# S5 mixer on one NeuronCore: tile 0's outputs with channels on the partitions, other gelu groups, earlier copies of u

## The chip, the cores and the metric

The kernel runs on one core of a Trainium2 chip. The metric is the device time of one execution in microseconds (us). All times below are us unless ns is written.

## What is computed

A trunk of two layers over x of [1, 256, 2048] in float32: differential attention and a squared-relu MLP, then the S5 mixer and a second MLP, each behind an RMS norm and added to the residual, and a final norm. The change touches the S5 mixer alone. Per group of 16 channels it is a diagonal complex state space of 64 states, read out and fed to a gated linear unit (GLU):

```
u = h.reshape(B, S, S5_GROUPS, S5_GROUP)
x_re, x_im = associative_scan(a, u @ b)        # over the 256 tokens
y = einsum(x_re, c_re) - einsum(x_im, c_im) + d_skip * h
g = gelu(y)
val, gate = split(g @ w_glu, 2)
out = val * sigmoid(gate)
```

## The kernel before

The 2048 channels are 16 tiles of 128 channels, and the 256 tokens are cut into 64 chunks of 4 tokens. Every tile is computed in a chunked form: matmuls give the end states of the chunks (`s5_e`, L1049, TensorE's line L1056), VectorE scans over the chunks (L1066) and makes the states that enter each chunk, and matmuls give the outputs (`s5_y`, L1078, TensorE's line L1089) from three terms: the tokens inside the chunk (`tt` with `u`) and the two parts of the entering state (`to` with `xp`). The tokens of a tile, `u`, are needed with token-in-chunk and channel on the partitions. `s5_u` (L1022) makes them for two tiles at a time: 8 matmuls onto one PSUM bank (TensorE, L1031) and 16 copies by ScalarE, each of 32 partitions and 128 elements (L1036).

`s5_y` puts the outputs into PSUM with 4 tokens x 32 channels on the partitions. So the gelu has to sort them: 16 instructions on ScalarE for a group of one or two tiles (L1096), each from one 32-partition strip to another and with a stride of 4 in what it writes. ScalarE then rounds the result (L1100), and VectorE makes the rounding's rest (`s5_rest`, L1107).

`glu_tile` (L1116, TensorE's line L1122) multiplies a tile's gelu, in full float32, with the first 512 columns of value and gate. It lags behind: tile 0 in step 2, tile 1 in step 3, none in step 4, and from step 5 on the tile three steps back.

The order of the work is written out by hand in `s5_phase` (L1129), and every engine keeps it. Step j issues: `s5_e` of tile j+1; `s5_rest` of tile j-3; in steps 0 and 1 eight warming matmuls (`keep_warm`, L320); `glu_tile`; the outputs of tile j; the copy of a decay table for tile j+4 (`s5_dk`, ScalarE, L1020); at the end of a group its gelus; in some steps `s5_u` of a later pair of tiles; and the fetch of tile j+4's tables on SP's queue (`s5_fetch`, L994). Before the steps, `s5_u` runs for tiles 4 to 7.

PSUM has 8 banks, given out in turn by `ring` (L88). In this phase the GLU sums hold four of them, `s5_y` takes banks 6 and 7 in turn, and `s5_e` and `s5_u` share banks 4 and 5, also in turn; a bank's new user waits until the old one has been read out:

```
rings["sd"], rings["y"] = [4, 5], [6, 7]
groups = [(0,), (1,), (2, 3), (4, 5), (6, 7), (8, 9), (10, 11), (12, 13), (14,), (15,)]
...
            if j in (2, 4, 6, 8):
                for _ in s5_u(j + 6, diag):
                    pass
```

The functions that the change touches, and what calls them:

Of the kernel before, what the change touches and what calls it, by code (L numbers as in the profile page):

```python
# [12 lines left out]
AF = mybir.ActivationFunctionType  # L13
# [3 lines left out]
P = 128  # L17
S = 256
# [4 lines left out]
KB = 4  # L23
# [12 lines left out]
L = 4  # L36
NCH = S // L
NJ = 16
Q = 4
# [18 lines left out]
def tile_trunk(  # L58
# [8 lines left out]
    act = nc.scalar  # L67
    pe = nc.tensor
# [11 lines left out]
    def nm(s):  # L80
        uid[0] += 1
        return f"{s}_{uid[0]}"
# [5 lines left out]
    def ring(kind):  # L88
        r = rings[kind]
        turn[kind] = (turn[kind] + 1) % len(r)  # L90
        return psum.tile([P, 512], F32, tag=f"bank{r[turn[kind]]}", name=nm(kind), bufs=1)
# [6 lines left out]
    def bank():  # L98
        return ring("sd")

    def tmp(shape, tag, bufs=None, dt=F32):
        if bufs is None:
            return sb.tile(shape, dt, tag=tag, name=nm(tag))
        return sb.tile(shape, dt, tag=tag, name=nm(tag), bufs=bufs)
# [10 lines left out]
    def tsc(o, a, s1, op0, s2=None, op1=None):  # L115
        if op1 is None:
            v.tensor_scalar(out=o, in0=a, scalar1=s1, scalar2=None, op0=op0)
        else:
            v.tensor_scalar(out=o, in0=a, scalar1=s1, scalar2=s2, op0=op0, op1=op1)
# [21 lines left out]
    def until(cond):  # L141
        while not cond():
            assert side
            pump()
# [79 lines left out]
    def new_accs():  # L224
        return [ring("acc") for _ in range(NT)]
# [94 lines left out]
    def keep_warm(n):  # L320

        if n == 0:
            return
        a = ring("acc")
        for _ in range(n):
            pe.matmul(a, x1[3].h[:, 0, 0:P], x1[3].h[:, 0:2], start=True, stop=True)

    def new_lhs(blk, tag):
        blk.hl = lp.tile([P, KB, 2, S], F32R, tag=tag, name=nm(tag))
        blk.h, blk.l = blk.hl[:, :, 0], blk.hl[:, :, 1]  # L330
# [659 lines left out]
    glu_lhs = [Lhs() for _ in range(NB)]  # L990
    tab, U, X, G = {}, {}, {}, {}
# [30 lines left out]
    def s5_u(j, diag=None, kind="sd"):  # L1022

        ps = ring(kind).rearrange("p (i s) -> p i s", s=S)
        for i in range(2):
            for t in range(NT):
                o, xs = ps[:, i, t * P:(t + 1) * P], xres[t][:, (j + i) * P:(j + i + 1) * P]
                if diag is None:
                    pe.transpose(o, xs, ident)
                else:  # L1030
                    pe.matmul(o, xs, diag[:, t], start=True, stop=True)  # L1031
        u = tmp([P, 2, Q, NCH], "vsb", bufs=4)
        pv = ps.rearrange("p i (k s) -> p i s k", s=L)
        for s in range(L):
            for q in range(Q):
                act.copy(u[32 * s:32 * s + 32, :, q], pv[32 * q:32 * q + 32, :, L - 1 - s])  # L1036
            yield s
        if diag is None:
            U[j] = u
        else:  # L1040
            U[j], U[j + 1] = u[:, 0], u[:, 1]

    def s5_scale(j, factor):
        u = U[j]
        uv = u.rearrange("p i q k -> p (i q) k")
        mult(uv, uv, factor[:, None, :].broadcast_to([P, 2 * Q, NCH]))
        U[j], U[j + 1] = u[:, 0], u[:, 1]

    def s5_e(j):  # L1049
        te, to, tt, ct = tab[j]  # L1050
        u, dk, xp = U[j], dks[j % 4], xps[j % 4]
        pe_ = bank().rearrange("p (i q k) -> p i q k", i=2, q=Q)
        for i in range(2):
            for q in range(Q):
                for h in (slice(0, GP), slice(GP, P)):
                    pe.matmul(pe_[h, i, q], te[:, i, q, h], u[:, q], start=True, stop=True)  # L1056
        sh = [P, 2, Q, NCH]
        tw = tmp([P, 2] + sh[1:], "c5")
        t1, t2 = tw[:, 0], tw[:, 1]
        mult(t1, pe_, ct[:, 0:1].broadcast_to(sh))  # L1060
        mult(t2, pe_, ct[:, 1:2].broadcast_to(sh))
        add(t1[:, 0], t1[:, 0], t2[:, 1])
        sub(t1[:, 1], t1[:, 1], t2[:, 0])
        zz = tmp(sh, "s2k", bufs=7)
        for i in range(2):
            v.tensor_tensor_scan(out=zz[:, i].rearrange("p q k -> p (q k)"), data0=dk.rearrange("p q k -> p (q k)"),  # L1066
                                 data1=t1[:, i].rearrange("p q k -> p (q k)"), initial=0.0,
                                 op0=ALU.mult, op1=ALU.add)
        n = NCH - 1
        shn = [P, 2, Q, n]  # L1070
        w1, w2 = tmp(sh, "s2k", bufs=7), tmp(sh, "s2k", bufs=7)
        mult(w1[:, :, :, 0:n], zz[:, :, :, 0:n], ct[:, 0:1, :, 0:n].broadcast_to(shn))
        mult(w2[:, :, :, 0:n], zz[:, :, :, 0:n], ct[:, 1:2, :, 0:n].broadcast_to(shn))
        sub(xp[:, 0, :, 1:], w1[:, 0, :, 0:n], w2[:, 1, :, 0:n])
        add(xp[:, 1, :, 1:], w1[:, 1, :, 0:n], w2[:, 0, :, 0:n])
        X[j] = xp

    def s5_y(grp):  # L1078

        n = len(grp)  # L1080
        py = ring("y").rearrange("p (j q k) -> p j q k", j=2, q=Q)
        for jj, j in enumerate(grp):
            te, to, tt, ct = tab[j]
            u, xp = U[j], X[j]
            for q in range(Q):
                terms = ((tt[:, q], u[:, q]), (to[:, 0, q], xp[:, 0, q]), (to[:, 1, q], xp[:, 1, q]))
                for m, (w_, d) in enumerate(terms):
                    for h in (slice(0, GP), slice(GP, P)):
                        pe.matmul(py[h, jj, q], w_[:, h], d, start=m == 0, stop=m == 2)  # L1089
            yield j  # L1090
            del U[j], X[j], tab[j]
        g = tmp([P, 2, S], "s2k", bufs=7)
        gv = g.rearrange("p j (k s) -> p j s k", s=L)
        for s in range(L):
            for q in range(Q):
                act.activation(gv[32 * q:32 * q + 32, 0:n, s], py[32 * s:32 * s + 32, 0:n, q], AF.Gelu_apprx_tanh)  # L1096
        blk, kk = glu_lhs[grp[0] // KB], grp[0] % KB
        if blk.h is None:
            new_lhs(blk, "x")
        act.copy(blk.h[:, kk:kk + n], g[:, 0:n])  # L1100
        for jj, j in enumerate(grp):
            G[j] = g[:, jj]
        rest.append((grp[-1], blk, kk, n, g))

    rest = []

    def s5_rest(j):  # L1107
# [21 lines left out]
    def s5_phase(norm):  # L1129
        until(lambda: norm.done)  # L1130
        act.activation(warm_act, warm_act, AF.Gelu_apprx_tanh)
        keep_warm(WARM[0])
        sel = wp.tile([P, 2, NT, P], F32, tag="wl", name="sel", bufs=LIVE)
        ar, diag = sel[:, 0], sel[:, 1]
        for t in reversed(range(NT)):
            tsc(ar[:, t], sela.rearrange("p s r -> p (s r)"), norm.rstd[:, t:t + 1], ALU.mult)
        for t in range(NT):
            act.activation(diag[:, t], ident, AF.Copy, scale=norm.rstd[:, t:t + 1])
        prs = bank()[:, 0:NCH]
        for t in range(NT):  # L1140
            pe.matmul(prs, ar[:, t], selb[:, t], start=(t == 0), stop=(t == NT - 1))
        keep_warm(WARM[1])
        s5_scale(0, prs)
        s5_scale(2, prs)
        s5_e(0)
        for j in (4, 6):
            for _ in s5_u(j, diag, "acc"):
                pass
        groups = [(0,), (1,), (2, 3), (4, 5), (6, 7), (8, 9), (10, 11), (12, 13), (14,), (15,)]
        ys = {}  # L1150
        for grp in groups:
            gen = s5_y(grp)
            for j in grp:
                ys[j] = (gen, j == grp[-1])
        glu = 0
        for j in range(NJ):
            if j + 1 < NJ:
                s5_e(j + 1)
            s5_rest(j - 3)
            if j < 2:  # L1160
                keep_warm(WARM[2])
            if j in (2, 3) or j >= 2 + LAG:
                if glu == 0:
                    A["v"], A["g"] = new_accs(), new_accs()
                glu_tile(glu)
                glu += 1
            gen, end = ys[j]
            next(gen)
            s5_dk(j + 4)
            if end:  # L1170
                for _ in gen:
                    pass
            if j in (2, 4, 6, 8):
                for _ in s5_u(j + 6, diag):
                    pass
            s5_fetch(j + 4)
            pump()
        while glu < NJ:
            prep(GLU0 + 16 + glu - NJ + LAG)
            glu_tile(glu)  # L1180
            glu += 1
        s5_rest(NJ)
# [212 lines left out]
```

## Time and profile before

| | |
|---|---|
| median of three runs | 2104.44 (2101.5 to 2106.57) |
| profiled execution, its time | 2101.04 |
| profiled execution, its span | 2099.3 |
| TensorE busy in the span | 2076.1 (99%) |
| VectorE, ScalarE, GpSimd busy | 1369.1, 1061.4, 122.9 |
| mean granted TensorE clock | 0.999 of full speed |

The profile's engines are PE (TensorE's matmuls), PEld (its weight loads), DVE (VectorE), ACT (ScalarE), POOL (GpSimd) and SP (the queue of most DMAs). A float32 matmul shows as two passes, so 24 matmuls are x48. `out<-in` names the tiles that an instruction writes and reads. A matmul's recorded duration contains its latency; what counts for the pace is the distance between starts, or the length of a whole row of passes.

### The profile page before, as it was taken

Reading aid. Unit: us, or ns where it says so; the run is one execution under the profiler, and the core shown is the slowest. Engines: PE = TensorE matmul, PEld = TensorE weight load, DVE = VectorE, ACT = ScalarE, POOL = GpSimd, SP = SyncE. Lnnn points to the kernel's source line nnn. Section 1 sums busy time; section 2 is a strip of 40 time slices with the busy share of each in tenths; the row PEclk is TensorE's granted clock in tenths of the full one; section 3 lists DMA queues with packets and bytes.
Section 4 is the critical chain, followed back from the end, with each engine's and each line's share of the span. In section 5 each row is a group of like instructions: output and inputs, shape, how many; then the busy total and the mean of one; then the engine's idle time right before and its main releaser. Section 6 shows DMA issues by size and latency. Waiting matters only on the chain.

```text
span 2099.3 us, 31788 instructions
## 1 busy us (share of the span) xinstructions
PE 2076.1 (99%) x12126; PEld 1763.8 (84%) x12126; DVE 1369.1 (65%) x2292; ACT 1061.4 (51%) x1640; POOL 122.9 (6%) x210
## 2 busy tenths in 40 slices
PE   8999999999999999999999999999999999999998
PEld 8899998888888888888887668888888888888886
DVE  5785656688678767767866865565556645645655
ACT  5545545555445444454566875444434434434443
POOL 2000200021021002100110000000000000000000
PEclk9999999999999999999999999999999999999999
DMA  7457765677776777687678765665565556555653
GB/s 244 157 193 241 248 178 184 214 229 267 237 240 233 273 238 222 225 276 235 208 266 310 274 215 187 200 201 199 189 195 189 189 193 191 178 204 181 200 192 131
DMA packets 230813, 452.57 MB, mean 216 GB/s; under 512 B 20818, under 2 KB 29348, under 8 KB 230660
## 3 DMA queue, kind: packets, MB, share of 16 engines
q1 hardware_dynamic: 217824, 415.29, 59.8%
q0 software_dynamic: 11440, 32.86, 4.9%
q10 hardware_dynamic: 1396, 2.39, 0.3%
q8 instruction: 95, 1.56, 0.3%
q14 instruction: 58, 0.48, 0.1%
HBM read 420.85 MB, written 41.68 MB: 220 GB/s over the span
## 4 chain that ended last, share of the span: by engine, by line
PE 91%; ACT 3%; DVE 3%; DMA 1%; issue 1%; SPq 0%; DVEq 0%; ACTq 0%
PE acc L265 21%; PE acc L201 15%; PE acc L202 15%; PE acc L203 15%; PE acc L269 11%; PE acc L1122 3%; PE acc L248 2%; PE acc L250 2%; PE acc L249 2%; DVE wl L113 1%; ACT wh L191 1%; PE y L1089 1%; ACT s2k L1096 1%; DMA raw<-in_a_w_in_dram 1%; ACT vsb L1036 1%
## 5 line engine op out<-in xcount | busy, mean ns | idle before, releaser
L113 DVE TENSOR_TENSOR wl<-raw,wh 128x1024 fp32r<-128x1024 f32 (+1 forms) x690 | 833.2, 1217 | 574.4 <-ACT wh L191 570.0
L191 ACT CAST wh<-raw 128x1024 fp32r<-128x1024 f32 (+1 forms) x690 | 712.9, 1047 | 631.0 <-PE acc L203 341.4
L201 PE MATMUL acc<-wh,x 128*128 128x512 f32 x832 | 326.8, 393 | 0.0
L203 PE MATMUL acc<-wh,x 128*128 128x512 f32 x832 | 324.0, 389 | 0.0
L202 PE MATMUL acc<-wl,x 128*128 128x512 f32 x832 | 324.0, 389 | 0.0
L265 PE MATMUL acc<-x,wh 128*128 128x512 f32 x1024 | 273.9, 394 | 2.8 <-DVE s2k L110 2.8
L265 PE MATMUL acc<-a,wh 128*128 128x512 f32 x1024 | 272.8, 393 | 0.0
L201 PE MATMUL acc<-wh,a 128*128 128x512 f32 x640 | 251.5, 393 | 0.0
L202 PE MATMUL acc<-wl,a 128*128 128x512 f32 x640 | 249.4, 390 | 0.1
L203 PE MATMUL acc<-wh,a 128*128 128x512 f32 x640 | 249.3, 390 | 0.0
L265 PEld LDWEIGHTS acc<-x,wh 128*128 128x128 f32 x1024 | 177.3, 189 | 28.9 <-DVE s2k L110 3.2
L265 PEld LDWEIGHTS acc<-a,wh 128*128 128x128 f32 x1024 | 177.3, 189 | 25.3 <-ACT s2k L1324 0.4
L203 PEld LDWEIGHTS acc<-wh,x 128*128 128x128 f32 x832 | 156.2, 188 | 32.9
L201 PEld LDWEIGHTS acc<-wh,x 128*128 128x128 f32 x832 | 156.3, 188 | 32.0 <-ACT vsb L1317 0.3
L202 PEld LDWEIGHTS acc<-wl,x 128*128 128x128 f32 x832 | 156.3, 188 | 31.8 <-issue 0.2
L269 PEld LDWEIGHTS acc<-a,wl 128*128 128x128 f32 x1024 | 152.8, 190 | 18.7
L269 PEld LDWEIGHTS acc<-x,wl 128*128 128x128 f32 x1024 | 152.4, 190 | 18.8
L269 PE MATMUL acc<-x,wl 128*128 128x256 f32 x1024 | 158.0, 282 | 0.0
L269 PE MATMUL acc<-a,wl 128*128 128x256 f32 x1024 | 157.5, 281 | 0.0
L248 PE MATMUL acc<-x,wh 128*128 128x256 f32 x512 | 148.4, 290 | 1.2 <-ACT wh L191 1.2
L249 PE MATMUL acc<-x,wh 128*128 128x256 f32 x512 | 145.4, 284 | 0.1
L250 PE MATMUL acc<-x,wl 128*128 128x256 f32 x512 | 145.5, 284 | 0.0
(246 smaller groups left out, 2105.8 us busy)
## 6 DMA issues: line engine op xcount, KB each, us to landing
raw<-in_mlp_w_dram SPq DMA_DIRECT2D x512, 512.0 KB
raw<-in_a_w_in_dram SPq DMA_DIRECT2D x94, 512.0 KB
raw<-in_b_w_glu_dram SPq DMA_DIRECT2D x64, 512.0 KB
raw<-in_a_w_out_dram SPq DMA_DIRECT2D x32, 512.0 KB
scr<-t POOLq DMA_DIRECT2D x32, 512.0 KB, 5.6
teo<-scr SPq DMA_DIRECT2D x32, 512.0 KB
t<-scr SPq DMA_DIRECT2D x16, 512.0 KB
pwr<-pwn SPq DMA_DIRECT2D x16, 256.0 KB
```

Of the source, the lines that this page charges most:

```text
L113: v.tensor_tensor(out=o, in0=a, in1=b, op=ALU.subtract)
L191: act.copy(h[:, sl], r[:, sl])
L201: pe.matmul(accs[t], lhs.h[:, k, ts], wh, start=first, stop=False)
L202: pe.matmul(accs[t], lhs.h[:, k, ts], wl, start=False, stop=False)
L203: pe.matmul(accs[t], lhs.l[:, k, ts], wh, start=False, stop=last)
L248: pe.matmul(o, wh[:, kk, cs], lhs.h[:, k], start=f and c % 2 == 0, stop=False)
L249: pe.matmul(o, wh[:, kk, cs], lhs.l[:, k], start=False, stop=False)
L250: pe.matmul(o, wl[:, kk, cs], lhs.h[:, k], start=False, stop=e and c % 2 == 1)
L265: pe.matmul(a[c], wh, lhs.hl[:, k].rearrange("p i s -> p (i s)"), start=first, stop=False)
L269: pe.matmul(a[c][:, S:], wl, lhs.h[:, k], start=False, stop=last)
L1036: act.copy(u[32 * s:32 * s + 32, :, q], pv[32 * q:32 * q + 32, :, L - 1 - s])
L1122: pe.matmul(accs[t], g[:, t * P:(t + 1) * P], raws[i][:, kk], start=j == 0, stop=j == NJ - 1)
```

## The change

Tile 0's outputs get a function of their own, `s5_y_direct`. Its matmuls have 32 columns of the stationary operand and write 32 channels x 64 chunks, for each of 4 tokens and 4 strips of channels; so channels lie on the partitions, and a single gelu over 128 partitions and 256 elements puts the tokens in order. Tiles 2 and 3 become groups of their own. `s5_u` for tiles 8 to 15 moves from steps 2, 4, 6, 8 to steps 1, 3, 5, 7, behind the outputs and gelus of that step.

```diff
+    def s5_y_direct(j):
+        te, to, tt, ct = tab[j]
+        u, xp = U[j], X[j]
+        py = ring("y")[:, 0:S].rearrange("p (s k) -> p s k", s=L)
+        for s in range(L):
+            cs = slice(32 * s, 32 * s + 32)
+            for q in range(Q):
+                terms = ((tt[:, q], u[:, q]), (to[:, 0, q], xp[:, 0, q]), (to[:, 1, q], xp[:, 1, q]))
+                for m, (w_, d) in enumerate(terms):
+                    pe.matmul(py[32 * q:32 * q + 32, s], w_[:, cs], d, start=m == 0, stop=m == 2,
+                              tile_position=(0, 32 * q))
+        yield j
+        del U[j], X[j], tab[j]
+        g = tmp([P, 2, S], "s2k", bufs=7)
+        act.activation(g[:, 0].rearrange("p (k s) -> p s k", s=L), py, AF.Gelu_apprx_tanh)
...
+        act.copy(blk.h[:, kk:kk + 1], g[:, 0:1])
+        G[j] = g[:, 0]
+        rest.append((j, blk, kk, 1, g))
...
-        groups = [(0,), (1,), (2, 3), (4, 5), (6, 7), (8, 9), (10, 11), (12, 13), (14,), (15,)]
+        groups = [(0,), (1,), (2,), (3,), (4, 5), (6, 7), (8, 9), (10, 11), (12, 13), (14,), (15,)]
...
-            gen = s5_y(grp)
+            gen = s5_y(grp) if grp[0] else s5_y_direct(0)
...
-            if j in (2, 4, 6, 8):
-                for _ in s5_u(j + 6, diag):
+            if j in (1, 3, 5, 7):
+                for _ in s5_u(j + 7, diag):
```

## Rows read from the trace of the kernel before

**Rows 1.** Windows view, S5 phase: stretch, length, busy time per engine, granted clock.

```profile
1129.70:1249.80 120.10, 115.27 (x1500) 75.93 (x1499) 94.44 (x182) 97.27 (x291) 0.00 (x0) 1.00 0.68 238
```

**Rows 2.** Chain of waits, S5 phase: start, length, engine, tile, line, instructions merged.

```profile
1175.77 1.15 PE sd L1056 x32
1176.92 3.63 PE acc L1122 x8
1180.55 1.55 PE y L1089 x48
1182.10 1.09 PE sd L1031 x8
1183.19 1.08 PE sd L1056 x32
```

**Rows 3.** Timeline of TensorE: start, length, line, tiles, shapes, [idle before <-releaser].

```profile
1146.89 0.62 PE L1089 MATMUL y<-bc,teo 128*64 128x64 f32 x8 [0.36 <-issue]
...
1151.27 3.70 PE L1122 MATMUL acc<-raw,s2k 128*128 128x512 f32 x8 [1.78 <-ACT s2k L1096]
...
1170.52 3.70 PE L1122 MATMUL acc<-raw,s2k 128*128 128x512 f32 x8 [2.15 <-ACT s2k L1096]
```

**Rows 4.** The same timeline: passes of the outputs now.

```profile
1142.07 0.29 PE L1089 MATMUL y<-vsb,t 128*64 128x64 f32 x4
1142.18 0.40 PE L1089 MATMUL y<-bc,teo 128*64 128x64 f32 x8
```

**Rows 5.** The same timeline: passes on 32-column strips, in the set-up of the tables.

```profile
1043.50 0.43 PE L927 MATMUL sd<-c,t 128*32 128x64 f32 x16
```

**Rows 6.** Timeline of ScalarE, steps 0, 1 and 3 to 5.

```profile
1146.57 4.64 ACT L1096 ACTIVATE s2k<-y 32x64 f32<-32x64 f32 x16
1151.25 0.40 ACT L1100 CAST x<-s2k 128x256 fp32r<-128x256 f32 x1
1151.56 0.39 ACT L1020 COPY s1k<-rr 128x252 f32<-128x252 f32 x1
...
1163.91 6.55 ACT L1096 ACTIVATE s2k<-y 32x128 f32<-32x128 f32 x16 [1.57 <-PE y L1089]
1170.50 0.62 ACT L1100 CAST x<-s2k 128x512 fp32r<-128x512 f32 x1
1171.02 0.40 ACT L1020 COPY s1k<-rr 128x252 f32<-128x252 f32 x1
1171.44 4.28 ACT L1036 COPY vsb<-sd 32x128 f32<-32x128 f32 x16
1175.74 0.40 ACT L1020 COPY s1k<-rr 128x252 f32<-128x252 f32 x1
```

**Rows 7.** One line's instructions (L466, 1257 to 1264): count, duration in ns min/median/max, shapes.

```profile
L466 ACT ACTIVATE a<-sd,gT x4: 474/475/476, 1258.5 to 1262.6; 128x256 fp32r<-128x256 f32 x4
```

**Rows 8.** Waits, 1120 to 1275: who waited for whom, us in total, times, longest.

```profile
PEld acc L201 <- ACT vsb L1317: 0.3, 1, 0.3
```

**Rows 9.** End of the program: TensorE's last matmul, then windows (granted clock third from last).

```profile
2089.48 0.39 PE L203 MATMUL acc<-wh,x 128*128 128x512 f32 x1
...
2092.00:2094.00 2.00, 0.00 (x0) 0.00 (x0) 1.71 (x6) 0.93 (x2) 0.75 (x1) 1.00 0.00 0
2094.00:2096.00 2.00, 0.00 (x0) 0.00 (x0) 0.28 (x1) 0.00 (x0) 0.00 (x0) 0.51 0.85 313
```

**Rows 10.** Timeline of TensorE at the program's start.

```profile
7.85 0.58 PE L248 MATMUL acc<-x,wh 128*128 128x256 f32 x1 [1.24 <-ACT wh L191]
...
9.60 0.41 PE L248 MATMUL acc<-x,wh 128*128 128x256 f32 x1
9.81 0.41 PE L249 MATMUL acc<-x,wh 128*128 128x256 f32 x1
...
12.17 0.28 PE L248 MATMUL acc<-x,wh 128*128 128x256 f32 x1
12.29 0.28 PE L249 MATMUL acc<-x,wh 128*128 128x256 f32 x1
```

More of the change, by code (lines that the diff above doesn't have):

```diff
@@ L1103, in s5_y @@
         rest.append((grp[-1], blk, kk, n, g))
+    def s5_y_direct(j):
[13 more added lines that the diff above has]
+        act.activation(g[:, 0].rearrange("p (k s) -> p s k", s=L), py, AF.Gelu_apprx_tanh)
+        blk, kk = glu_lhs[j // KB], j % KB
+        if blk.h is None:
+            new_lhs(blk, "x")
+        act.copy(blk.h[:, kk:kk + 1], g[:, 0:1])
+        G[j] = g[:, 0]
+        rest.append((j, blk, kk, 1, g))
     rest = []
```

## The prediction

> **What bounds the kernel now.** I first read the windows view over the S5 phase, from its first warming matmul to the first matmul of the next product: 120.1 us, of which TensorE is busy 115.3, ScalarE 97.3 and VectorE 94.4 [rows 1]. TensorE sets the pace, but with under 5 us to spare: whatever delays it comes out at the end of the phase, and what follows is a chain of matmuls, so a shift here moves the end of the program by as much.
>
> Next the chain of waits in this stretch, to see what a step is made of. A plain step on TensorE is the state matmuls of the next tile ("e", L1056, 1.08), the GLU product of an older tile (L1122, 3.63), the outputs ("y", L1089, 1.55) and, in four steps, the transposes of a pair of tiles ("u", L1031, 1.09) [rows 2]. Then TensorE's timeline, for where it stands still: 0.36 before y of tile 1, 1.78 before the first GLU product, 2.15 before the third [rows 3]. Both long waits end with a gelu. Removing everything that these rows show is worth 4.3 us, 0.2% of the time, which is also about what a measurement of this kernel can tell from no change.
>
> **The change, part by part.**
>
> *Outputs of tile 0.* Removed are 48 passes (24 matmuls, two passes each) in 1.55; added are 96 passes (48 matmuls) onto strips of 32 columns of the array. In the outputs of now, 4 passes take 0.29 and 8 take 0.40 [rows 4]: passes alternate between the two halves, so 4 more passes are 2 more rounds, 55 ns a round. The kernel has passes on 32-column strips in one place, L927: 16 passes in 0.43 [rows 5], but there neighbours go to different strips. In the new loop the six passes of one sum follow one another on the same strip, then come six on the next. If passes start in program order, as they do in all these rows, only the last of six overlaps with the first of the next: 5 rounds of 55 ns and some 10 ns to move on, 0.29 for each of 16 sums, 4.6 in all. The bounds are four strips fully in parallel (24 rounds, 1.3) and no overlap (96 rounds, 5.3). I take 4.6, since program order is what the rows show: 3.05 more than now. Nothing covers it: TensorE works in order, and e of tile 2, the warming matmuls and y of tile 1 stand behind it.
>
> By the Trainium skill ("TensorEngine Tiling", Theoretical Speedup) a stationary operand of 32 columns or fewer allows up to a fourfold gain, as tiles run independently. By that rule the new outputs take the lower bound and the sum falls by 3.3.
>
> *One gelu for tile 0.* Removed are 16 gelus of 32x64, 4.68 from the first to the cast behind them [rows 6]; added is one of 128x256. The nearest row is a scaled copy of the same shape out of PSUM, 0.475 [rows 7]; the gelus, which write with a stride as the new one does, go from 4.64/16 for 64 elements to 6.55/16 for 128 [rows 6], 1.9 ns an element, which gives 0.65 for 256. Either way ScalarE gains about 4.0. The gelu of tile 1 doesn't start 4 us earlier for it, as it waits for y of tile 1, which the longer y of tile 0 pushes back. The first GLU product loses its wait of 1.78, since its gelu is done long before.
>
> *Single gelus for tiles 2 and 3.* Two times 16 gelus of 32x64 in place of 16 of 32x128: 2 x 4.68 + 2 x 0.31 against 6.59 + 0.52 [rows 6], 2.9 more on ScalarE, but tile 2's are done a step earlier, so the third GLU product loses its 2.15. The outputs of tiles 0 to 3 now take a bank each; every y finds its bank's gelu finished.
>
> *The copies of u one step earlier.* This is the part that decides. The transposes of a pair of tiles go into one of two PSUM banks that they share, in turn, with e of every tile. After u of step j comes e of tile j+2 in the other bank and e of tile j+3 in u's own: it has to wait until ScalarE has copied all of u out. Before, u stands in steps 2, 4, 6, 8, behind the step's y, and in steps 4, 6 and 8 no gelu of that step is ahead of its copies. Even so there is little room: the copies of step 4 run from 1171.44 to 1175.72 [rows 6], and e of tile 7, the next in that bank, starts at 1175.77 [rows 2]. That a matmul waits for ScalarE to read out its bank is also seen where the next product waits for the eviction of the values [rows 8].
>
> After, u stands in steps 1, 3, 5 and 7, which all end a group: the gelus of that step come first on ScalarE's queue, they wait for the y just issued, and the copies wait behind them. From the end of y ScalarE needs gelu + cast + copies: 6.59 + 0.52 + 4.28 = 11.4 for a pair, 4.68 + 0.31 + 4.28 = 9.3 for a single tile [rows 6]. TensorE meanwhile has only u, one e, one GLU product and one y: 1.09 + 1.08 + 3.63 + 1.55 = 7.35; behind step 3 there is no GLU product (step 4 has none), so 3.7 [rows 2]. New waits of TensorE: step 1, 9.3 - 7.35 = 1.95 (before e of tile 4); step 3, 5.6 (tile 6); steps 5 and 7, 4.05 each (tiles 8 and 10); 15.7 in all. Everything on TensorE is queued behind these e, y included, so ScalarE can't work ahead either. VectorE's share is hidden: it waits for the same e. Moved with u are only its 8 passes and 16 copies; SP's and POOL's queues pass unchanged, and the fetches issued per step have a step or more in hand.
>
> *The sum without the clock:* 15.7 + 3.05 - 4.3 = +14.5 (between +11.1 and +15.2 by the bounds of the outputs).
>
> *The clock.* TensorE has not stood still for 5.6 us in this phase. At the end of the program the granted clock is still 1.00 in the stretch up to 2094 and 0.51 in the next, with the last matmul at 2089.48 [rows 9]: it falls to the lower of its levels (1.2 of 2.4 GHz) some 4 us behind the last work. After the 2.15 of now it doesn't fall: the phase reads 1.00 throughout [rows 1]. So the wait of 5.6 is likely to bring a fall, those of 4.05 stand on the edge. What one costs is bounded below by nothing and priced by the program's start: identical matmuls follow each other at 0.21 until about 11.6 and at 0.12 behind [rows 10], from 7.85 on 3.7 us of work, half of it lost: 1.9. I count one fall: +16.3 or so.
>
> By the Trainium skill ("TensorE: Matmul & The Clock Gate", HAM oscillation) a loop with idle gaps between its bursts of matmuls can run each burst at half rate. By that rule the three long gaps each cost a fall, and the sum is 3.8 higher; the trace bears out the fall at its end, and no gap in its middle is long enough to test it.
>
> The profiled execution took 2101.04, the median of three runs is 2104.44. The sum gives 2117.3 against the first and 2120.7 against the second; I predict a median, so 2120.7.
>
> **Rivals.**
> - *The waits come, the clock holds:* +14.5, 2118.9. For it: single waits under some length are harmless now. Against it: 5.6 is longer than the lag seen at the end of the program. Chance 0.22.
> - *The clock falls in each of the three long waits:* 14.5 + 3 x 1.9 = +20.2, 2124.6. For it: 4.05 is close to the lag at the end. Chance 0.15.
> - *Not slower: u is copied out in time.* The place is e of tiles 4, 6, 8 and 10. If the bank is free when TensorE comes by, only the outputs (+3.05) and the lost waits (-4.3) remain: -1.2, 2103.2; with the outputs at their lower bound -4.5, 2099.9. It decides from the point where gelu and cast together stay under 3.1 us behind y; now they take 7.1 for a pair. Against it are the durations, which hardly vary, and that e of tile 7 starts right behind the copies already; for it is only that I order the queues by reading the code. Chance 0.13, of which 0.03 for a gain over 0.2%.
>
> **How the numbers follow.** The forecast, four bank waits and one fall of the clock, has 0.50. Slower by over 0.2%: 0.50 + 0.22 + 0.15 = 0.87; within 0.2%: 0.10; faster: 0.03. The range begins at the forecast's mechanism with the outputs at their lower bound and no fall, +11.1, against a quiet execution, so about 2113, and ends with three falls and a little for the spread of the runs, 2126; it leaves out the not-slower rival and little else.
>
> **What would show it.** In the profile of the changed kernel TensorE waits for the copies of u (L1036's line) at e four times, about 2, 5.6, 4 and 4 us, in place of its waits for gelus; in the windows view its idle time in the phase grows by some 11 us and the phase from 120 to about 136. The outputs of tile 0 show 96 passes in about 4.6, its gelu one instruction of 0.5 to 0.65. The granted clock dips once behind e of tile 6. I am wrong if e of tiles 6, 8 and 10 start right behind the work before them; then the time is that of now.

## The result, and the profile after

| | before | after |
|---|---|---|
| median, four runs each | 2103.68 | 2121.85 |
| range | 2101.5 to 2106.57 | 2120.73 to 2123.01 |
| profiled execution, its time | 2101.04 | 2123.01 |
| profiled execution, its span | 2099.3 | 2121.2 |
| mean granted TensorE clock | 0.999 | 0.993 |

The changed kernel is slower: ratio 1.009, 95% interval 1.0078 to 1.0103, 18.2 us by the medians. The profiled execution is the slowest of its four, and the one of before (2101.04) lies below all four of its column; so the two traces stand 21.9 apart, more than the medians do. What follows accounts for these 21.9. All ratios of this document leave out one execution of the last experiment, which took 3465.81 at a granted clock of 0.557.

The S5 phase, windows view, answering to [rows 1]:

```profile
1129.50:1271.70 142.20, 125.18 (x1548) 81.75 (x1548) 94.58 (x183) 96.05 (x293) 0.00 (x0) 0.92 0.58 200
```

It begins 0.2 earlier than before and ends 21.9 later, 142.2 long in place of 120.1: all of the 21.9 is here, and the matmuls behind it are only shifted. ScalarE and VectorE have as much work as before; TensorE stands still for 17.0 instead of 4.8, and its granted clock is 0.92 in the mean.

Where it stands still: the waits of TensorE, 1120 to 1295 (who waited for whom, us in total, times, longest).

```profile
PE sd L1056 <- ACT vsb L1036: 16.5, 4, 5.9
PE acc L1145 <- ACT s2k L1096: 0.5, 1, 0.5
```

And TensorE's timeline (L1145 is now the line of the GLU product), a GLU product at full clock first, then the four waits, each with what ran behind it; answers to [rows 3].

```profile
1151.02 3.70 PE L1145 MATMUL acc<-raw,s2k 128*128 128x512 f32 x8
1158.39 1.15 PE L1056 MATMUL sd<-vsb,teo 128*64 128x64 f32 x32 [2.12 <-ACT vsb L1036]
1159.47 5.40 PE L1145 MATMUL acc<-raw,s2k 128*128 128x512 f32 x8
...
1175.89 1.98 PE L1056 MATMUL sd<-vsb,teo 128*64 128x64 f32 x32 [5.90 <-ACT vsb L1036]
1177.80 4.95 PE L1145 MATMUL acc<-raw,s2k 128*128 128x512 f32 x8
...
1195.86 1.98 PE L1056 MATMUL sd<-vsb,teo 128*64 128x64 f32 x32 [4.21 <-ACT vsb L1036]
1197.76 5.21 PE L1145 MATMUL acc<-raw,s2k 128*128 128x512 f32 x8
...
1216.10 1.98 PE L1056 MATMUL sd<-vsb,teo 128*64 128x64 f32 x32 [4.24 <-ACT vsb L1036]
1218.01 5.32 PE L1145 MATMUL acc<-raw,s2k 128*128 128x512 f32 x8
```

The four e that wait are those of tiles 4, 6, 8 and 10, and the releaser is the line of u's copies. None of these e reads what those copies write (tile 4, for one, reads a u that was made before the steps); the two have only the PSUM bank in common. ScalarE's timeline of step 5 shows why: gelus, cast and copies stand in one queue, and the gelus begin only when y is done; answers to [rows 6].

```profile
1184.34 6.51 ACT L1096 ACTIVATE s2k<-y 32x128 f32<-32x128 f32 x16 [7.78 <-PE y L1089]
1190.89 0.62 ACT L1100 CAST x<-s2k 128x512 fp32r<-128x512 f32 x1
1191.53 4.27 ACT L1036 COPY vsb<-sd 32x128 f32<-32x128 f32 x16
```

ScalarE was idle for 7.8 ahead of these gelus: only when it had ended the copies of step 3 could TensorE go on with e, the GLU product and y, and for that y the gelus waited. The two engines wait for each other in turn.

Behind the waits the same instructions take longer: e 1.98 in place of 1.15 behind the last three, a GLU product 5.0 to 5.4 in place of 3.70 behind all four. The windows view gives the reason in the granted clock (third from last):

```profile
1156.30:1158.40 2.10, 0.01 (x2) 0.01 (x2) 1.14 (x3) 1.99 (x9) 0.00 (x0) 1.00 0.63 177
1159.50:1160.50 1.00, 1.00 (x4) 0.61 (x3) 0.91 (x2) 0.96 (x4) 0.00 (x0) 0.68 0.09 16
1170.00:1173.00 3.00, 0.00 (x0) 0.00 (x0) 2.97 (x6) 2.85 (x11) 0.00 (x0) 1.00 0.94 287
1173.00:1175.90 2.90, 0.01 (x2) 0.01 (x2) 1.30 (x4) 2.76 (x12) 0.00 (x0) 0.59 1.03 401
1175.90:1181.00 5.10, 5.10 (x37) 3.28 (x38) 3.05 (x6) 0.67 (x2) 0.00 (x0) 0.56 0.34 139
1195.90:1201.00 5.10, 5.10 (x36) 3.26 (x37) 3.09 (x6) 0.63 (x2) 0.00 (x0) 0.52 0.49 198
1216.10:1222.00 5.90, 5.90 (x38) 3.62 (x39) 3.81 (x7) 0.68 (x2) 0.00 (x0) 0.56 0.41 156
```

These are four falls to half (1.2 of 2.4 GHz), one for each wait, the first of them after a wait of only 2.1 and when work had already resumed. By the durations they cost three times (1.98 - 1.15) for e and (1.70 + 1.25 + 1.51 + 1.62) for the GLU products, 8.6 together.

Tile 0's outputs (L1115) and their gelu (L1120), TensorE's and ScalarE's timelines:

```profile
1141.28 0.30 PE L1115 MATMUL y<-vsb,t 128*32 128x64 f32 x2
...
1142.08 0.22 PE L1115 MATMUL y<-vsb,t 128*32 128x64 f32 x1
1142.11 0.25 PE L1115 MATMUL y<-bc,teo 128*32 128x64 f32 x2
1142.14 0.24 PE L1115 MATMUL y<-vsb,t 128*32 128x64 f32 x1
1142.16 0.25 PE L1115 MATMUL y<-bc,teo 128*32 128x64 f32 x2
...
1143.81 0.42 PE L1115 MATMUL y<-bc,teo 128*32 128x64 f32 x6
1144.15 1.15 PE L1056 MATMUL sd<-vsb,teo 128*64 128x64 f32 x32
...
1146.39 0.64 ACT L1120 ACTIVATE s2k<-y 128x256 f32<-128x256 f32 x1
```

The same two places in the kernel before:

```profile
1141.46 0.34 PE L1089 MATMUL y<-vsb,t 128*64 128x64 f32 x4
...
1143.12 1.10 PE L1056 MATMUL sd<-vsb,teo 128*64 128x64 f32 x32
```

From the first pass to the next e are 2.87; before, the same stretch was 1.66, so +1.2. The sum of the parts: 16.5 for u, 8.6 for the clock, 1.2 for the outputs, less 4.3 of the waits that went: 22.0, against 21.9 in the spans.

### The profile page after: what moved, and what is told of

It is laid out like the page before. It is cut to its first block, busy times and chain, and to the rows that moved or that the text cites. A ratio compares the mean times of both kernels' runs of the same rounds, so it can differ in the third digit from the quotient of the medians.

```text
span 2121.2 us, 31887 instructions
## 1 busy us (share of the span) xinstructions
PE 2085.7 (98%) x12174; PEld 1770.1 (83%) x12174; DVE 1369.6 (65%) x2293; ACT 1060.6 (50%) x1642; POOL 123.0 (6%) x210
## 4 chain that ended last, share of the span: by engine, by line
PE 92%; ACT 3%; DVE 2%; DMA 1%; issue 1%; SPq 0%; DVEq 0%; ACTq 0%
PE acc L265 21%; PE acc L202 15%; PE acc L203 15%; PE acc L201 15%; PE acc L269 11%; PE acc L248 3%; PE acc L250 3%; PE acc L249 3%; PE acc L1145 2%; ACT s2k L1096 1%; DVE wl L113 1%; ACT vsb L1036 1%; PE y L1089 1%; PE sd L1056 1%; ACT wh L191 1%
```

## The experiments

My theory was that u's place is all of it: the bank that u shares with e, behind gelus in ScalarE's queue, and the falls of the clock that these waits bring. The rival was that the new outputs and the two further groups of gelus load the engines beyond what there is.

**u back in its steps, the rest of the change kept.**

```diff
-            if j in (1, 3, 5, 7):
-                for _ in s5_u(j + 7, diag):
+            if j in (2, 4, 6, 8):
+                for _ in s5_u(j + 6, diag):
```

> The changed kernel with u of tiles 8 to 15 back in steps 2, 4, 6 and 8; the new outputs of tile 0 and the single gelus stay. Bank theory (e of a later tile waits for ScalarE to copy u out of its bank): the four waits of 16.5 us go but for some 2 us before e of tile 5 or 7, no fall of the clock inside the phase, and the time is within 3 us of the kernel before, likeliest 1 below it. Rival (the new outputs and the two more gelu groups load TensorE and ScalarE beyond what there is): at least 8 us of the 18 stay.

Measured: 2102.06 against 2102.11 before, ratio 0.9997 (0.9987 to 1.0006). All of the loss is gone. TensorE's waits for the copies in the phase:

```profile
1167.35 1.15 PE L1056 MATMUL sd<-vsb,teo 128*64 128x64 f32 x32 [2.13 <-ACT vsb L1036]
1177.51 1.15 PE L1056 MATMUL sd<-vsb,teo 128*64 128x64 f32 x32 [0.26 <-ACT vsb L1036]
```

The single gelus of tiles 2 and 3 don't remove the 2.15 of [rows 3], they move it: the GLU product doesn't wait any more, but in step 2 the gelus of tile 2 now stand ahead of the copies of tiles 8 and 9, and e of tile 5 waits 2.13 for these copies.

The totals don't tell a small gain from none; the traces show one of 0.9 in the phase. From its first warming matmul to the last 24 passes of the GLU are 109.46 in the kernel before, 131.61 in the changed one and 108.54 here. But this profiled execution has a fall of the granted clock elsewhere, at 818, which the last section comes back to.

**u moved, and nothing else.** The kernel before with the last two lines of the diff only (the reverse of the one above).

> The kernel before with only u of tiles 8 to 15 moved to steps 1, 3, 5 and 7; outputs of tile 0 and the gelu groups as before. Bank theory: waits at e of tiles 4, 6, 8 and 10 of about 4.8, 7.8, 4.1 and 4.1 us, the first two longer than in the changed kernel as the first 16 gelus and the paired gelus of tiles 2 and 3 are ahead of the copies; with three or four falls of the clock at 2 us each the time is 22 to 27 above the kernel before, so above the changed kernel too. Rival (u's place alone is harmless, it needs the other parts): less than 8 above.

Measured: 2128.11, ratio 1.0121 (1.0106 to 1.0136), 26.0 above the kernel before, with waits of 4.90, 7.98, 4.24 and 4.23:

```profile
1161.50 1.82 PE L1056 MATMUL sd<-vsb,teo 128*64 128x64 f32 x32 [4.90 <-ACT vsb L1036]
1180.97 1.98 PE L1056 MATMUL sd<-vsb,teo 128*64 128x64 f32 x32 [7.98 <-ACT vsb L1036]
1201.06 1.98 PE L1056 MATMUL sd<-vsb,teo 128*64 128x64 f32 x32 [4.24 <-ACT vsb L1036]
1221.34 1.98 PE L1056 MATMUL sd<-vsb,teo 128*64 128x64 f32 x32 [4.23 <-ACT vsb L1036]
```

Together with the first experiment this rules the rival out: u's move alone costs more than the whole change, and the other parts, which relieve ScalarE ahead of the first two sets of copies, give some of it back, 5.3 by the spans and 6.5 by the ratios (the waits are 4.9 longer here).

**Work of no use in the waits.** The changed kernel with matmuls whose result nobody reads, ahead of the e that wait, onto the other of the two banks of the outputs.

```diff
+    def fill(n):
+        py = ring("y")
+        turn["y"] = (turn["y"] - 1) % len(rings["y"])
+        for _ in range(n):
+            pe.matmul(py[:, 0:P], ident, ident, start=True, stop=True)
...
+            if j in (3, 5, 7, 9):
+                fill(7 if j == 3 else 15)
             if j + 1 < NJ:
                 s5_e(j + 1)
```

> The changed kernel with matmuls of no use to the result before the four e that wait (7 at step 3, 15 at steps 5, 7 and 9, each of 128x128 in float32 onto the outputs' other bank), so that TensorE is busy for most of each wait. Clock theory (falls of the granted clock cost 8.5 of the 21.9 us of the profiled execution): the granted clock stays at 1.00 through the phase, the waits for u stay and are taken up by the added work, and the time is 5 to 9 us below the changed kernel. Rival (the half clock costs little, since ScalarE sets the pace behind each wait): within 2 us of the changed kernel.

Measured: 2115.38, ratio 1.0063 (1.0048 to 1.0078), where the changed kernel has 1.009: 5.7 us less by the ratios, 7.4 by the spans (2113.8 and 2121.2). The windows view over the phase, and over two of the old waits:

```profile
1125.00:1270.00 145.00, 140.39 (x1702) 98.30 (x1701) 101.23 (x197) 101.30 (x300) 0.00 (x0) 1.00 0.64 225
1170.00:1176.00 6.00, 4.29 (x52) 4.10 (x54) 3.69 (x8) 5.73 (x21) 0.00 (x0) 1.00 0.97 347
1189.00:1194.00 5.00, 4.31 (x57) 4.12 (x57) 0.58 (x2) 4.72 (x18) 0.00 (x0) 1.00 0.98 340
```

The clock holds, and e takes 1.15 again:

```profile
1175.33 1.15 PE L1056 MATMUL sd<-vsb,teo 128*64 128x64 f32 x32 [1.12 <-ACT vsb L1036]
1193.24 1.15 PE L1056 MATMUL sd<-vsb,teo 128*64 128x64 f32 x32 [0.69 <-ACT vsb L1036]
```

So some 6 to 7 of the loss are the clock by these totals, and some 13 are the waits themselves, which no filler removes: the sum without the clock, 16.5 + 1.2 - 4.3 = 13.4, is what is measured here (13.3 above the kernel before by the medians). The phase alone bears out the larger price of the durations: from the first warming matmul to the last 24 GLU passes it takes 123.13, 8.5 less than in the changed kernel and 13.7 more than before.

**Copies first.** The changed kernel with u issued ahead of the step's gelus.

```diff
+            if j in (1, 3, 5, 7):
+                for _ in s5_u(j + 7, diag):
+                    pass
             if end:
                 for _ in gen:
                     pass
-            if j in (1, 3, 5, 7):
-                for _ in s5_u(j + 7, diag):
-                    pass
```

> The changed kernel with u still in steps 1, 3, 5 and 7, but issued ahead of the gelus of the step, so that ScalarE copies first. Bank theory: e of tiles 4, 8 and 10 no longer wait for the copies; gelus are 4.3 us later, so waits of GLU products for gelus come in their place, about 2 for tile 1 and 3.8 each for tiles 4 and 6; 6 to 11 us above the kernel before. Rival (the transposes' early place on TensorE is what costs, not the copies' place in ScalarE's queue): as the changed kernel, 16 or more above.

Measured: 2113.43, ratio 1.0056 (1.0041 to 1.0071), 11.3 above the kernel before.

TensorE's waits of more than 1 in the phase:

```profile
1159.17 3.70 PE L1145 MATMUL acc<-raw,s2k 128*128 128x512 f32 x8 [1.84 <-ACT s2k L1096]
1169.87 1.15 PE L1056 MATMUL sd<-vsb,teo 128*64 128x64 f32 x32 [1.88 <-ACT vsb L1036]
1188.20 5.40 PE L1145 MATMUL acc<-raw,s2k 128*128 128x512 f32 x8 [3.71 <-ACT s2k L1096]
1207.13 6.62 PE L1145 MATMUL acc<-raw,s2k 128*128 128x512 f32 x8 [3.71 <-ACT s2k L1096]
```

Tiles 4, 8 and 10 no longer wait for the copies, tile 6 for 1.88 instead of 5.90, with TensorE's order unchanged: it is the copies' place behind the gelus that held the bank. But ScalarE has 11.4 to do behind the y of a step that ends a pair, and whichever of the two comes second is late: here the GLU products wait for gelus, 1.84, 3.71 and 3.71. Two of them fall into half clock (5.40 and 6.62 for 3.70), and e of tile 6 still waits, for which the expectation had no price; together they bring the time a little over the expected 6 to 11.

**The new outputs alone.** The kernel before with the new outputs and single gelu of tile 0; gelu groups and u's steps as before (`groups` keeps `(2, 3)`).

> The kernel before with only the new outputs of tile 0 and their single gelu; groups of gelus and steps of u as before. If these outputs take the 2.9 us that the changed kernel shows (1.2 more than before) and the wait before the first GLU product goes (1.8), the time is 1 to 2 us below the kernel before; the wait before the third GLU product stays at 2. If they cost what the prediction said (4.6), the time is 1 above it or more.

Measured: 2100.66 against 2103.16, ratio 0.9992 (0.9984 to 1.0001): of the size expected, and not told apart from no change. From its first warming matmul to the last 24 GLU passes the phase takes 108.13, 1.3 less than before. The wait before the first GLU product is gone, the one before the third stays:

```profile
1169.79 3.70 PE L1145 MATMUL acc<-raw,s2k 128*128 128x512 f32 x8 [2.13 <-ACT s2k L1096]
```

**The same with terms outside, strips inside.**

```diff
-            for q in range(Q):
-                terms = ((tt[:, q], u[:, q]), (to[:, 0, q], xp[:, 0, q]), (to[:, 1, q], xp[:, 1, q]))
-                for m, (w_, d) in enumerate(terms):
+            for m in range(3):
+                for q in range(Q):
+                    w_, d = ((tt[:, q], u[:, q]), (to[:, 0, q], xp[:, 0, q]), (to[:, 1, q], xp[:, 1, q]))[m]
                     pe.matmul(py[32 * q:32 * q + 32, s], w_[:, cs], d, start=m == 0, stop=m == 2,
                               tile_position=(0, 32 * q))
```

> As the kernel with the new outputs alone, with the loops over terms and strips swapped, so that neighbouring passes go to the four strips in turn. If strips run side by side when neighbours differ (as in L927), the 96 passes take about 1.4 to 1.7 us in place of 2.9 and the time falls by another 1 us at most; if the pace of starts is the limit (24 ns or more a pass as in the changed kernel), they take 2.5 as before and the time is the same.

Measured: 2100.07, ratio 0.9984 (0.9975 to 0.9993), faster than before. From the first pass to the start of the last, in TensorE's timeline:

```profile
1142.33 0.32 PE L1115 MATMUL y<-vsb,t 128*32 128x64 f32 x8
1142.48 0.60 PE L1115 MATMUL y<-bc,teo 128*32 128x64 f32 x16
...
1143.68 0.41 PE L1115 MATMUL y<-bc,teo 128*32 128x64 f32 x16
```

96 passes now begin within 1.6 (1142.33 to 1143.9), as long as the 48 of before took. The gain over the loops of the change, 0.6 by the medians, lies within the intervals; the phase takes 107.66, 0.5 less than with those loops.

**u later instead of earlier.** The changed kernel with the swapped loops and u two steps later than before, three later than in the change (the expectation calls it one step later than before; the steps that it lists are these):

```diff
-            if j in (1, 3, 5, 7):
-                for _ in s5_u(j + 7, diag):
+            if j in (4, 6, 8, 10):
+                for _ in s5_u(j + 4, diag):
```

> The changed kernel with the swapped loops and u one step later than before instead of one earlier: steps 4, 6, 8 and 10, for tiles 8, 10, 12 and 14. Bank theory: with the durations of the rows no e waits for u and no GLU product for a gelu up to tile 11, a wait of about 1 stays before y of tile 4, and the time is 3 to 3.5 us (0.15%) below the kernel before, the best of all. Rival (another wait comes, such as e of tile 8 for its u): at or above the kernel before.

Measured: 2098.73 against 2103.16, ratio 0.9981 (0.9972 to 0.999): the fastest of all, though its interval overlaps that of the one before. The longest waits that are left in its phase:

```profile
1164.58 0.67 PE L1089 MATMUL y<-bc,teo 128*64 128x64 f32 x8 [0.82 <-DVE bc L113]
1232.92 3.70 PE L1145 MATMUL acc<-raw,s2k 128*128 128x512 f32 x8 [0.55 <-ACT s2k L1096]
```

No e waits for copies any more. The first set of copies, of tiles 8 and 9, now runs when the gelus of tiles 1 to 3 are done, and the third GLU product doesn't wait for a gelu either. The first warming matmul and the last 24 GLU passes in the kernel before:

```profile
1129.73 4.24 PE L326 MATMUL acc<-x 128*128 128x512 f32 x18
...
1239.19 10.57 PE L1122 MATMUL acc<-raw,s2k 128*128 128x512 f32 x24
```

And here:

```profile
1131.66 4.24 PE L326 MATMUL acc<-x 128*128 128x512 f32 x18
...
1238.10 10.57 PE L1145 MATMUL acc<-raw,s2k 128*128 128x512 f32 x24
```

That is 106.44 in place of 109.46, 3.0 less, as expected, and 1.2 less than in the run before this one. So in the traces the single gelus pay off once u is out of their way; by the totals of the executions that last step is not told apart from noise.

## Why the prediction was right, and where its terms were off

*The mechanism and its places were right.* The waits are at e of tiles 4, 6, 8 and 10, released by the copies of u: 2.12, 5.90, 4.21 and 4.24, where the prediction had 1.95, 5.6, 4.05 and 4.05 (16.5 against 15.7). The experiments that undo and isolate the move show that it is u's place, and the one that swaps copies and gelus shows that it is ScalarE's queue. That the shared bank ties the two is read from the code and from the releaser in the trace; no run gave u a bank of its own.

*The outputs of tile 0 were sized too high*, 4.6 predicted, 2.87 measured from the first pass to the next e. The step that failed is that passes start in program order, so that only the last pass of a sum can overlap with the next sum. In the trace the recorded starts of two sums alternate (from 1142.08 on, `vsb,t` of one between `bc,teo` of the other), a sum of six passes every 0.142, where five rounds of 55 ns and the step to the next were to make 0.29. With the loops swapped neighbouring passes go to different strips, and 96 of them begin within 1.6, near the lower bound of 1.3 that the prediction worked out. By the Trainium skill ("TensorEngine Tiling", Theoretical Speedup) a stationary operand of 32 columns allows up to a fourfold speedup. Against the 5.3 of no overlap, an estimate of the prediction, the changed loops gain about twofold (2.7) and the swapped ones 3.3-fold (1.6).

*The clock was sized too low.* One fall of 1.9 was predicted; the profiled execution has four, which cost 8.6. The price of one was nearly right (2.1 each), their number was not. The step that failed is the lag of 4 taken from the end of the program as the point from which a wait brings a fall: the waits of 4.2, which the forecast let pass, brought one each, and so did the one of 2.1, as did two of 3.71 in the run with the copies first. So the rival with three falls was the better account of the clock, though not of the time (2124.6). By the Trainium skill ("TensorE: Matmul & The Clock Gate", HAM oscillation) bursts of matmuls behind idle gaps can run at half rate. The trace agrees for all three long gaps: 0.56, 0.52 and 0.56 granted in the 5 to 6 us behind 5.90, 4.21 and 4.24.

The two errors have opposite signs but don't balance: 1.8 too much for the outputs, 6.7 too little for the clock and 0.8 too little for the waits. The sum is 22.0 as measured in the profiled executions, where the prediction had 16.3. That the forecast of 2120.7 came within 1.2 of the measured 2121.85 is in part luck: the medians moved by only 18.2, and the median that the forecast started from, 2104.44 of three runs, stood 0.8 above the one of four. How many falls the executions without a profile had, no run shows.

*The gelu terms* held: one gelu of 128x256 takes 0.64 (0.65 predicted), and the waits of 1.78 and 2.15 for gelus are gone. But the second is not gained: with u where it was it comes back as a wait of e for the copies, which the prediction, laying out only the changed order, didn't look for.

## What to carry to other kernels

When a producer is moved earlier on one engine, look at the buffer that it takes, not only at the work that it brings forward: here two PSUM banks in turn serve two users, so the move brings forward the point at which the bank must be free again, while the engine that frees it still has a gelu ahead in its queue. The price can be read before building, as the consumer's queue time behind the event that starts it, less the producer's work up to the next use of that bank. And a wait on TensorE can cost more than its length: add what the work behind it may lose at half clock, here 2.1 in the mean behind each of the four.

## What the runs showed of the hardware that I had not expected

A wait of about 2 us on TensorE is followed by a fall of the granted clock in some executions and not in others, and its length doesn't tell which: 2.12 before e of tile 4 was followed by one (0.68 and less from 1159.5 on, a microsecond into the work behind it), while 2.15 in the kernel before and 2.13 in the kernel with u put back were not. The same shows far ahead of the phase, where TensorE waits for VectorE in every run. In the kernel with u put back, TensorE's timeline and the windows view:

```profile
818.02 0.95 PE L265 MATMUL acc<-x,wh 128*128 128x512 f32 x2 [1.86 <-DVE s2k L110]
```

```profile
818.00:820.00 2.00, 1.98 (x6) 1.70 (x7) 1.28 (x3) 0.95 (x3) 1.92 (x4) 0.59 1.04 406
```

There 1.86 was followed by a fall, and so was 1.88 with u later (0.53); 1.95 in the changed kernel and 2.30 with the filler were not (1.00). Such a fall is part of the time of an execution without having to do with the change.

Float32 passes on 32-column strips overlap with those of the next sum even where six passes in a row go to one strip: 96 passes start within 2.7 us (1141.28 to about 1144.0), 28 ns apart in the mean and six every 0.142 us once they run, against the 55 ns that the prediction took for a round on one strip; with neighbours on different strips they start 16 ns apart.
